# Relative-position softmax on one core: rows of one late chunk are dealt to the DMA engines by list

## The chip, the cores and the metric

The kernel runs on one core of a Trainium2 chip. The core has a vector engine (DVE), a scalar engine (ACT), a general engine (POOL), a synchronizing engine (SP) that here issues the transfers, and 16 DMA engines that move the bytes between the chip's memory (HBM) and the core's own memory (SBUF, 128 partitions). The metric is the device time of one execution in microseconds. TensorE does nothing in this kernel.

## The reference

Logits of shape 2 x 8 x 2112 x 2112 (float32, 285 MB) get a bias that depends on the distance of row and column alone, clipped to 16 on both sides, and then a softmax along the last axis:

```python
rel = pos[:, None] - pos[None, :]
rel_clipped = np.clip(rel, -max_rel, max_rel) + max_rel
bias = rel_bias[:, rel_clipped].copy()
logits = logits + bias[None, :, :, :]
logits = logits - logits.max(axis=-1, keepdims=True)
exp = np.exp(logits)
return (exp / exp.sum(axis=-1, keepdims=True)).astype(np.float32)
```

Each element is read once and written once: 571 MB in all.

## The kernel before

There are 2 x 8 x 2112 = 33,792 rows of 2112 numbers. Each of the 128 partitions takes 264 consecutive rows (`ROWS`), and works through them in 44 chunks of six rows (`N`, `R`). So a chunk is a tile of 128 partitions x 12,672 numbers, 6.3 MB, and one partition's share of it is one contiguous run of 50,688 bytes in HBM; this text calls that a full row of the transfer. Four buffers `X[0]` to `X[3]` hold four chunks (`NBUF`); chunk n lives in buffer n mod 4.

For each chunk DVE adds the bias to the six rows and finds each row's negated maximum (`add`, line 177, one instruction per row on line 181), ACT takes the exponential and the row's sum (`exps`, line 186), and DVE multiplies by the reciprocal sums in two halves of three rows (`scale`, line 195). The bias strip of four chunks is copied from PSUM to `F` once per four chunks (`strip`, line 173).

SP issues the loads and stores, all into one hardware queue per DMA engine, in this order. It first issues six one-row-per-partition loads for chunk 0 and the loads of chunks 1 to 3 (lines 98 to 103). Chunk 0 is stored in two parts: five of its six rows by one transfer (line 219), and the sixth by 17 small transfers (`FAN`, lines 41 to 48 and 221 to 232), which take k = 15, 14, 13, ... partitions, nine apart, so that DMA engine 0 gets 17 of these small rows and engine 15 none. The loop on line 233 then alternates: the store of the next chunk (which waits on `scaled` for six rows), a wait for the store before it to have landed (`st[b]`), and the load of the chunk that takes that buffer. POOL does the waiting for the parts of chunk 0's store (lines 114 to 117) and then adds 16 to `st[0]`, which lets SP issue the first reload. After the loop, lines 238 to 241 store chunks 41 and 42 whole and chunk 43 in two halves of three rows. Lines 242 to 244 wait until everything has landed.

So the transfers on the queue alternate store and load through the whole kernel, and at the end they are: store 40, load 43, store 41, store 42, and the two halves of 43. A transfer over 128 partitions gives each of the 16 DMA engines eight full rows.

## Time and profile before

| | |
|---|---|
| median of 3 runs | 1331.54 us (1331.24 to 1331.57) |
| the profiled execution | 1331.3 us |
| its span, first to last instruction | 1329.5 us |
| DVE busy | 976.7 us (73%) |
| ACT busy | 575.2 us (43%) |
| POOL busy | 0.4 us |
| moved by DMA | 571.12 MB, mean 430 GB/s |

Beside the table, the profile offers views that the prediction quotes. The page shows, in 40 slices of the span, the share of time in which the 16 DMA engines were busy (a 9 is 90% or more), and for each DMA queue its packets, MB and share. A row on a stretch gives its start and end, its length, the busy time of DVE, ACT and POOL with the number of instructions, the granted TensorE clock, the busy share of the DMA engines and the GB/s moved. A row of a timeline gives start, duration, engine, source line, operation, what is written and read, and, in brackets, idle time before it. "SPq" is SP's instruction stream: its issue of a transfer takes some tenths of a microsecond, while the transfer itself goes on in the queue. A row of the waits gives who waited for whom, the total, the number and the longest.

### The profile page before, as it was taken

To read this page: it belongs to the slowest core of one execution; us is meant where nothing else is said; L and a number is where in the kernel's file an instruction comes from. 1 tells how busy PE (TensorE), PEld (TensorE's weight loads), DVE (VectorE), ACT (ScalarE), POOL (GpSimd) and SP (SyncE) were. 2 spreads that over 40 slices of the span, in tenths; PEclk is the share of its full clock that TensorE was granted. 3 is DMA by queue.
4 is the path that set the end of the run, shared out by engine and by line. 5 is a ranking of instruction groups with operands and counts; after the bars stand their busy time and mean duration, and the time that the engine had idled before them with its cause. 6 is when DMAs were issued, how large, how long until landed. Compare 5 with 4: busy or idle time off the path is not lost. (4 is left out here: it accounts for less than half of the span.)

```text
span 1329.5 us, 2477 instructions
## 1 busy us (share of the span) xinstructions
DVE 976.7 (73%) x911; ACT 575.2 (43%) x539; POOL 0.4 (0%) x6
## 2 busy tenths in 40 slices
DVE  5998767777877776787778767677877776687772
ACT  2565333444444343345444333444444343345440
POOL 0000000000000000000000000000000000000000
DMA  9999999999999999999999999999999999999997
GB/s 391 427 426 424 436 430 433 438 433 435 432 435 435 433 436 430 436 433 435 430 433 439 433 433 427 439 435 432 433 432 438 430 433 430 436 430 436 438 432 337
DMA packets 13939, 571.12 MB, mean 430 GB/s; under 512 B 1648, under 2 KB 1776, under 8 KB 1776
## 3 DMA queue, kind: packets, MB, share of 16 engines
q1 hardware_dynamic: 13792, 570.96, 99.5%
q10 hardware_dynamic: 144, 0.14, 0.1%
q14 instruction: 3, 0.02, 0.0%
HBM read 285.61 MB, written 285.47 MB: 430 GB/s over the span
## 5 line engine op out<-in xcount | busy, mean ns | idle before, releaser
L181 DVE CUSTOM_DVE_ANT_0 X<-X,F 128x2112 f32<-128x2112 f32 x264 | 605.2, 2354 | 302.0 <-DVEq L85 302.0
L190 ACT ACTIVATE X<-X,nmax 128x2112 f32<-128x2112 f32 x264 | 541.7, 2052 | 538.2 <-ACTq L85 516.4
L202 DVE TENSOR_SCALAR X<-X,rec 128x2112 f32<-128x2112 f32 x264 | 332.5, 1316 | 13.2
L190 ACT ACT_TABLE_LOAD x11 | 14.1, 1283 | 185.8 <-ACTq L85 185.8
L190 ACT ACTIVATION_READ_ACCUMULATOR X<-X,nmax 128x1 f32 x264 | 49.2, 186 | 0.0
L175 DVE COPY F<-M 128x2135 f32 x11 | 26.1, 2375 | 6.6 <-DVEq L85 6.6
L181 DVE DVE_READ_ACCUMULATOR2_ANT nmax<- 128x1 f32 x264 | 21.7, 82 | 0.0
L198 DVE RECIPROCAL rec<-tot 128x3 f32<-128x3 f32 x88 | 15.0, 170 | 0.0
L146 DVE TENSOR_TENSOR F<-F 128x264 f32<-128x264 f32 x1 | 0.4, 435 | 4.9 <-DMA F<-in_rel_bias_dram 4.9
L167 DVE COPY M<-F 128x1848 f32<-128x1848 f32 x1 | 2.1, 2077 | 0.0
L133 DVE TENSOR_SCALAR ip<-ip 128x8 int32<-128x8 int32 x1 | 0.2, 172 | 1.3 <-POOL ip L113 1.3
L150 DVE TENSOR_REDUCE rbS<-F 128x33 f32<-128x264 f32 x1 | 0.6, 610 | 0.0
L164 DVE TENSOR_TENSOR M<-F 128x264 f32<-128x264 f32 x1 | 0.4, 441 | 0.0
L156 DVE TENSOR_TENSOR F<-F,rbS 128x264 f32<-128x264 f32 x1 | 0.4, 426 | 0.0
L143 DVE TENSOR_SCALAR F<-F 128x8 f32<-128x8 f32 x4 | 0.4, 167 | 0.0
L169 DVE COPY M<-rbS 128x247 f32<-128x247 f32 x1 | 0.4, 406 | 0.0
L154 DVE TENSOR_SCALAR F<-F,rbS 128x8 f32<-128x8 f32 x1 | 0.2, 231 | 0.0
L160 DVE SCALAR_TENSOR_TENSOR F<-F,rbS 128x8 f32<-128x8 f32 x1 | 0.2, 227 | 0.0
L155 DVE TENSOR_SCALAR F<-F,rbS 128x8 f32<-128x8 f32 x1 | 0.2, 225 | 0.0
L161 DVE SCALAR_TENSOR_TENSOR F<-F,rbS 128x8 f32<-128x8 f32 x1 | 0.2, 221 | 0.0
L136 DVE TENSOR_TENSOR F<-ip 128x8 f32<-128x8 int32 x1 | 0.2, 167 | 0.0
L139 DVE TENSOR_TENSOR F<-ip 128x8 f32<-128x8 int32 x1 | 0.2, 167 | 0.0
(9 smaller groups left out, 1.2 us busy)
## 6 DMA issues: line engine op xcount, KB each, us to landing
X<-in_logits_dram SPq DMA_DIRECT2D x43, 6336.0 KB, 44.7
out_dram<-X SPq DMA_DIRECT2D x42, 6336.0 KB, 52.8
X<-in_logits_dram SPq DMA_DIRECT2D x6, 1056.0 KB, 12.6
out_dram<-X SPq DMA_DIRECT2D x2, 3168.0 KB, 21.9
out_dram<-X SPq DMA_DIRECT2D x1, 5280.0 KB, 34.9
F<-in_rel_bias_dram ACTq DMA_DIRECT2D x1, 132.0 KB, 6.4
out_dram<-X SPq DMA_DIRECT2D x1, 123.8 KB
out_dram<-X SPq DMA_DIRECT2D x1, 115.5 KB
```

The costliest lines, as they stand in the source:

```text
L143: then(v.tensor_scalar(out=m, in0=dp, scalar1=0.0, scalar2=None, op0=op))
L146: then(v.tensor_tensor(out=view(F, 0, [[W, H], [1, W]]), in0=view(F, 0, [[W, H], [1, W]]), in1=view(F, SC + 3 * PB, [[1, H], [0, W]]), op= ...
L150: then(v.tensor_reduce(out=rbS[:, :], in_=view(F, 0, [[1, W], [W, H]]), axis=mybir.AxisListType.X, op=ALU.add))
L156: then(v.tensor_tensor(out=view(F, 0, [[W, PB], [1, W]]), in0=view(F, SC + 2 * PB, [[1, PB], [0, W]]), in1=view(rbS, W - 1, [[0, PB], [-1, ...
L164: then(v.tensor_tensor(out=view(M, U, [[ROWS, PB], [1, W]]), in0=view(F, 0, [[W, PB], [1, W]]), in1=view(F, SC + 8 * PB, [[1, PB], [0, W]] ...
L167: then(v.tensor_copy(out=view(M, U + W, [[ROWS, PB], [1, ROWS - W]]), in_=view(F, SC + 7 * PB, [[1, PB], [0, ROWS - W]])))
L169: then(v.tensor_copy(out=M[:, 0:U], in_=low.to_broadcast([P, U])))
L175: v.tensor_copy(out=F[:, :], in_=M[:, bass.ds(ROWS - STEP - j, FW)]).then_inc(dve, 1)
L181: v.tensor_tensor_reduce(out=x, in0=x, in1=F[:, STEP - 1 - r : STEP - 1 - r + S], scale=-1.0, scalar=BIG, op0=ALU.add, op1=ALU.min, accum_ ...
L190: nc.scalar.activation(out=x, in_=x, func=EXP, scale=-1.0, bias=nmax[:, r : r + 1], accum_out=tot[:, r : r + 1],).then_inc(expd, 1)
L198: v.reciprocal(out=rec[:, r0 : r0 + HALF], in_=tot[:, r0 : r0 + HALF]).then_inc(inv, 1)
L202: v.tensor_scalar_mul(out=x, in0=x, scalar1=rec[:, r : r + 1]).then_inc(scaled, 1)
```

## The change

The store of chunk 41, the last but two, is cut into parts. A partition p with p mod 8 in `OWN` = 0, 1, 2, 4, 5, 6 is stored by one of six SP transfers, each of 16 partitions that lie eight apart. The other 32 partitions (p mod 8 is 3 or 7) are stored by POOL with indirect transfers: each takes n partitions of the buffer, beginning at p0 and `lap` apart, and an index per partition that says which of the output's 5632 blocks of 12,672 numbers it goes to. An index past the last block (`FAR`) is skipped. `PLAN` lists five such transfers, each with the positions i whose index is kept: none of 112; 5 to 15 of 16 (partitions 43, 51, ...), twice, from 3 and from 7; eight of 16; and two of 16 (partitions 19 and 23). Together they keep 32 positions, each partition once.

POOL builds the five index columns in `sel` at the start, by an iota and two to five selects each, before it waits for chunk 0's store. Later it waits on `ready`, which SP raises when chunk 41 is scaled, at the place where SP issued the store before, and issues the five transfers. SP's wait for that store's landing counts six transfers now, and one more wait, on `soft`, covers the indirect ones. Nothing else is changed; DVE and ACT run the same instructions.

```diff
+    OWN = [0, 1, 2, 4, 5, 6]
+    PLAN = [
+        (112, 0, 1, []),
+        (16, 3, 8, range(5, 16)), (16, 7, 8, range(5, 16)),
+        (16, 3, 4, [0, 1, 2, 3, 6, 7, 8, 9]), (16, 9, 1, [10, 14]),
+    ]
+    FAR = 1 << 20
...
+        for w, (n, p0, lap, keep) in enumerate(PLAN):
+            col = sel[:, w : w + 1]
+            step(g.iota(col, pattern=[[0, 1]], base=p0 * N + N - 3, channel_multiplier=lap * N))
+            a, b = (min(keep), max(keep)) if keep else (P, P)
+            cuts = [(-a, 1, ALU.is_ge), (b, -1, ALU.is_ge)]
+            cuts += [(-i, 1, ALU.not_equal) for i in range(a, b) if i not in keep]
+            for base, mul, op in cuts:
+                g.wait_ge(pool, made[0])
+                step(g.affine_select(out=col, in_=col, pattern=[[0, 1]], base=base, channel_multiplier=mul,
+                                     compare_op=op, fill=float(FAR)))
+        take(g, pool, made[0])
         take(nc.gpsimd, main, 16)
         take(nc.gpsimd, fan[0], 16 * ((len(FAN) + 1) // 2))
         take(nc.gpsimd, fan[1], 16 * (len(FAN) // 2))
         nc.gpsimd.sem_inc(st[0], 16)
+        take(g, ready, 1)
+        blocks = out.rearrange("b h s t -> (b h s t)").rearrange("(n c) -> n c", c=R * S)
+        late = X[(N - 3) % NBUF]
+        LX = list(late.ap[0])[0]
+        for w, (n, p0, lap, keep) in enumerate(PLAN):
+            g.indirect_dma_start(
+                out=blocks, out_offset=bass.IndirectOffsetOnAxis(ap=sel[0:n, w : w + 1], axis=0),
+                in_=bass.AP(tensor=late.tensor, offset=late.offset + p0 * LX, ap=[[lap * LX, n], [1, R * S]]),
+                in_offset=None, bounds_check=P * N - 1, oob_is_err=False,
+            ).then_inc(soft, 16)
...
-        for n in range(N - NBUF + 1, N - 1):
-            store(n * R, n % NBUF)
+        take(nc.sync, scaled, R)
+        nc.sync.sem_inc(ready, 1)
+        for o in OWN:
+            nc.sync.dma_start(
+                out=bass.AP(
+                    tensor=out.tensor, offset=out.offset + (o * ROWS + (N - 3) * R) * S,
+                    ap=[[8 * ROWS * S, P // 8], [1, R * S]],
+                ),
+                in_=bass.AP(
+                    tensor=late.tensor, offset=late.offset + o * LX, ap=[[8 * LX, P // 8], [1, R * S]]
+                ),
+            ).then_inc(st[(N - 3) % NBUF], 16)
+        store((N - 2) * R, (N - 2) % NBUF)
         store((N - 1) * R, (N - 1) % NBUF, 0, HALF, landed)
         store((N - 1) * R, (N - 1) % NBUF, HALF, R - HALF, landed)
         for b in range(NBUF - 1):
-            take(nc.sync, st[(N + b) % NBUF], 16)
+            take(nc.sync, st[(N + b) % NBUF], 16 * len(OWN) if b == 1 else 16)
+    nc.sync.wait_ge(soft, nc.sync.to_reg(16 * len(PLAN)), synchronizes=[nc.sync.lower_ap(out)])
     nc.sync.wait_ge(landed, nc.sync.to_reg(32), synchronizes=[nc.sync.lower_ap(out)])
```

More of the change, by code (lines that the diff above doesn't have):

```diff
@@ L40 @@
     BIG = 3.0e38
+    OWN = [0, 1, 2, 4, 5, 6]
[5 more added lines that the diff above has]
+    FAR = 1 << 20
+    assert sorted(p0 + lap * i for n, p0, lap, keep in PLAN for i in keep) == [
+        p for p in range(P) if p % 8 not in OWN
+    ]
     LANES = 9
@@ L56 @@
     rec = io.tile([P, STEP], FP32, tag="rec", name="rec")
+    sel = io.tile([P, len(PLAN)], I32, tag="sel", name="sel")
     ip = io.tile([P, 3, PB], I32, tag="ip", name="ip")
@@ L79 @@
         dve = nc.alloc_semaphore("dve")
+        ready = nc.alloc_semaphore("ready")
+        pool = nc.alloc_semaphore("pool")
+        soft = tc.alloc_semaphore("soft")
         main = nc.alloc_semaphore("main")
@@ L113, with step @@
         nc.gpsimd.iota(ip[:, 2], pattern=[[1, PB]], base=0, channel_multiplier=0).then_inc(idx, 1)
+        g = nc.gpsimd
+        made = [0]
+        def step(ins):
+            made[0] += 1
+            ins.then_inc(pool, 1)
+        for w, (n, p0, lap, keep) in enumerate(PLAN):
[9 more added lines that the diff above has]
+        take(g, pool, made[0])
         take(nc.gpsimd, main, 16)
```

## The prediction

> **What bounds the kernel now.** I read three views: the page's DMA rows (is the queue ever empty?), the stretches at the end (how does it run dry?) and the timelines of SP and DVE (does compute hold a store back?). The page first:

> ```profile
> span 1329.5 us, 2477 instructions
> DMA  9999999999999999999999999999999999999997
> q1 hardware_dynamic: 13792, 570.96, 99.5%
> X<-in_logits_dram SPq DMA_DIRECT2D x43, 6336.0 KB, 44.7
> out_dram<-X SPq DMA_DIRECT2D x42, 6336.0 KB, 52.8
> ```

> All loads and stores are in queue q1, and it keeps 16 engines busy 99.5% of the span: bytes set the time, not DVE. Only the last slice is short of 9. The stretches (us, DVE busy, ACT busy, POOL busy, PEclk, DMA share, GB/s) show why:

> ```profile
> 130.00:500.00 370.00, 270.59 (x249) 157.14 (x149) 0.00 (x0) 1.00 1.00 434
> 1244.00:1305.00 61.00, 43.82 (x41) 25.78 (x24) 0.00 (x0) 1.00 1.00 432
> 1320.00:1321.00 1.00, 0.00 (x0) 0.00 (x0) 0.00 (x0) 1.00 0.77 329
> 1321.00:1322.00 1.00, 0.00 (x0) 0.00 (x0) 0.00 (x0) 1.00 0.59 253
> 1322.00:1323.00 1.00, 0.00 (x0) 0.00 (x0) 0.00 (x0) 1.00 0.41 177
> 1323.00:1324.00 1.00, 0.00 (x0) 0.00 (x0) 0.00 (x0) 1.00 0.41 177
> 1324.00:1325.00 1.00, 0.00 (x0) 0.00 (x0) 0.00 (x0) 1.00 0.24 101
> 1325.00:1326.00 1.00, 0.00 (x0) 0.00 (x0) 0.00 (x0) 1.00 0.18 76
> 1326.00:1327.00 1.00, 0.00 (x0) 0.00 (x0) 0.00 (x0) 1.00 0.06 25
> 1327.00:1328.50 1.50, 0.00 (x0) 0.00 (x0) 0.00 (x0) 1.00 0.04 17
> ```

> Times 16, the shares say that 12, 9, 7, 7, 4, 3 and 1 engines still work from 1320 on: the kernel ends with one engine alone. A full row (one partition's chunk, 50,688 bytes) costs an engine, at 434/16 = 27.1 GB/s, 1.87 us. The trace's packet records, which no view prints, say which engine is late. On one engine packets follow each other without a gap; every transfer gives each engine it uses its packets and then one of 4 bytes; and the 17 one-row transfers of chunk 0 give engine 0 seventeen packets, then 15, 14, 13, 12, 11, 10, 8, 7, 6, 5, 4, 3, 2, 1, 0, which names each chain. I followed the chains to the end:

> ```
> engine    0       1       2       3       4       5       6       7
> ends   1326.19 1325.95 1324.60 1325.72 1328.12 1324.18 1322.34 1321.89
> engine    8       9      10      11      12      13      14      15
> ends   1321.72 1320.89 1324.09 1320.88 1320.90 1320.87 1321.23 1321.99
> ```

> Their mean is 1323.2, so perfect balance would be worth 4.9 us. Engines 0 to 5 are late mostly by the one-row packets. Two have a cause of their own, seen in the time of their packets over the nominal one (1.872 us for a full row; sums in us, from the records):

> ```
> stretch       120-500   500-900   900-1300
> engine 4         1.15      1.80       1.46   (some 5 ns in every packet)
> engine 10        0.00      1.12       0.99   (ten single packets)
> engine 9         0.00      0.00       0.00
> ```

> **The change, part by part.**

> *Rows per engine.* The store of chunk 41 gives each engine eight rows. The six SP transfers give row i of 16 to engine i, six rows each. The lists name 32 more rows by position: engine 4 none, 0 to 3 one each, 5, 11, 12, 13, 15 two, 6 to 10 and 14 three (4 + 10 + 18 = 32). If position i is engine i there too, an engine's end moves by (count - 2) x 1.87:

> ```
> engine    0       1       2       3       4       5       6       7
> after  1324.32 1324.08 1322.73 1323.85 1324.38 1324.18 1324.21 1323.76
> engine    8       9      10      11      12      13      14      15
> after  1323.59 1322.76 1325.96 1320.88 1320.90 1320.87 1323.10 1321.99
> ```

> Engine 4 leaves the end, gaining 3.74; engine 10, late here and yet given a third row, is next. Last packet 1328.12 to 1325.96: -2.16 us. That one-row transfers go by position is in the records (engine 15 has none of the 17); that indirect ones do is not. [...]

> *Price of an indirect row.* None in this trace. Nearest: 1.87, the full row on q1. Below it nothing: a busy engine already moves at the rate of the 434 GB/s row. Above: the longest full-row packet of the records, 2.88. I take 1.87, since the 10,880 rows of that size in the records have a median of 1.87. At 2.88, engine 10 ends at 1324.09 - 3.74 + 3 x 2.88 = 1328.99, 0.9 later than now. Those ends, -2.2 and +0.9, go into the range.

> *The last load comes later.* SP and DVE at the end:

> ```profile
> 0.96 3.27 SPq L99 DMA_DIRECT2D X<-in_logits_dram  x6
> ...
> 1238.15 0.35 SPq L89 DMA_DIRECT2D X<-in_logits_dram  x1
> 1244.93 60.38 SPq L93 DMA_DIRECT2D out_dram<-X  x4
> 1271.08 3.78 DVE L202 TENSOR_SCALAR X<-X,rec 128x2112 f32<-128x2112 f32 x3
> 1283.08 2.36 DVE L181 CUSTOM_DVE_ANT_0 X<-X,F 128x2112 f32<-128x2112 f32 x1 [8.22 <-DVEq L85]
> 1300.77 0.17 DVE L198 RECIPROCAL rec<-tot 128x3 f32<-128x3 f32 x1
> 1301.09 3.78 DVE L202 TENSOR_SCALAR X<-X,rec 128x2112 f32<-128x2112 f32 x3
> ```

> Chunk 41 is scaled at 1244.9, while q1 still holds the store of 40 and the load of 43; the indirect rows go in between these, so each engine ends the load of 43 by count x 1.87 later. By the records engine 4 ends it last, at 1282.43, and engine 10 at 1279.18; after: engine 10 at 1284.8, the others by 1283.2. DVE starts chunk 43 some 2.3 later than 1283.08, and its first half, scaled and issued from 1301 on, goes out near 1303.3. A packet needs about 1.4 us from issue (first issue 0.96, first packet 2.35 in the records): 1304.7. The first engine needs it at 1305.86. Hidden, with 1.2 to spare; what it would cost without that cover is idle time on engines 11 to 13, which have 5 us in hand. The second half has over 5 us of cover.

> *SP and POOL.* Six issues take the place of one:

> ```profile
> 44.01 12.37 SPq L223 DMA_DIRECT2D out_dram<-X  x17
> 83.32 0.39 SPq L89 DMA_DIRECT2D X<-in_logits_dram  x1
> 1.13 0.14 POOL L113 IOTA ip<- 128x8 int32 x1
> SPq L244 <- DMA out_dram<-X: 14.6, 1, 14.6
> ```

> 12.37/17 = 0.73 each, 4.4 us, done by 1249.4. Behind them on SP is only the store of 42, whose data come at 1271.08 + 3.78 = 1274.9: nothing waits. POOL gets 5 iotas and 15 selects, 20 x 0.14 and a wait before each select, 3 to 6 us, ahead of its release of the first reload, which reached SP at 83.3: hidden by some 75 us of idle POOL, and all of those 6 us would show on the load of chunk 4 without it. The new wait of POOL for SP has only the five indirect issues behind it, whose rows any time up to 1300 would do; I bound five issues by SP's 0.35 to 0.73 each, 2 to 4 us, and let even 20 us pass. The first of them names no row, so it costs POOL time alone. SP's new wait for the indirect rows stands before the one for the last halves, which holds 14.6 us anyway: nothing. Nine or ten more completion packets of 9 ns per engine, and one more semaphore clear at the end: +0.15 together, an estimate from the records.

> *Sum.* -2.16 + 0.15 = -2.0 on the profiled execution's 1331.3, so 1329.3. That execution lies 0.24 under the median of 1331.54; against the median it is -2.2, or 0.17%. About 0.2% (2.7 us, 1328.9 and 1334.2) is what a measurement here can tell from no change.

> **Rivals.**

> *1. Engine 10 is not late.* Its 2 us came from ten stretched packets; the times of before can't tell if it is late in each run, as engine 4 hides it. Then the end is engine 4, 0 or 6 near 1324.4: -3.7 + 0.15, 1327.8. For it: the stretches fell on other engines in other spans. Against: five other engines carry a third row, and any may be hit instead.

> *2. Mixing stretches packets.* Indirect stores run beside a load, and q1's rows stretch as they did early on:

> ```profile
> 90.00:112.00 22.00, 20.61 (x19) 12.22 (x12) 0.00 (x0) 1.00 1.00 408
> ```

> (434 - 408)/434 x 22 = 1.3 us more per engine: 1330.6. Against: the queue here has long been in step, and other mixed stretches keep 432.

> *3. No rebalancing.* The rows do not go by position. If the refused indices drop out before rows are dealt, each list starts at engine 0: engines 0 and 1 get four rows, engine 4 three, and the last ends at 1328.12 + 1.87 = 1329.99, 1333.3. If each engine gets two, nothing changes: 1331.5. [...]

> *4. Slower: the rows eight apart run at half speed.* In the six SP transfers engines i and i + 4 read partitions 32 apart. If two engines reading such partitions halve each other, six rows cost 6 x 1.87 = 11.2 more: 1340.5. It decides from 0.8 more per row: then engine 10 ends 2.66 after 1328.12, at 2.67 per row. [...]

> **How the numbers follow.** Forecast, 1329.3 (1328.6 to 1330): 0.36. Rival 1: 0.34. Rival 2: 0.10. Rival 3: 0.09. Rival 4: 0.11. Range: rival 1 with 0.3 off, 1327.5, up to rival 3's 1333.3, which takes in the upper price of an indirect row (1331.3 + 0.9 + 0.15 = 1332.4); it leaves out rival 4 and some edges. The likeliest alone: 1328.6 to 1330.0. Faster by over 0.2%: nearly all of rival 1 and a quarter of the forecast, 0.41. Slower: rival 4 and a trace of others, 0.12. Within: 0.47.

> **What would show it.** A queue beside q1 with 32 rows of 50,688 bytes, 1.6 MB; shares after 1320 that stay high and then fall within 2 to 3 us; the last packet near 1326, engine 10's; DVE's first instruction of chunk 43 at 1284 to 1286; SP's issues of both last halves not behind an idle queue. Wrong would be: indirect rows well over 1.9 us, the six transfers slower than 11.2 us per engine, or a late engine that the list loads.

## The result: 0.57% slower

The changed kernel takes 1338.86 us (median of five, 1337.06 to 1342.12); the kernel before took 1331.26 beside it (1331.09 to 1331.57). The ratio is 1.0057, with a 95% interval of 1.0041 to 1.0074: slower, by 7.6 us. The profiled execution is one of the quicker ones, 1337.28 us, 5.98 more than the profiled execution of before. 1329.3 was forecast, and the range ended at 1333.3: the prediction was wrong, in sign too. What happened is in the main its rival 4, rows eight apart at half speed.

The page of the changed kernel, the lines that answer to those of before:

```profile
span 1335.5 us, 2534 instructions
DMA  9999999999999999999999999999999999999998
q1 hardware_dynamic: 13840, 569.33, 99.3%
q0 software_dynamic: 256, 1.62, 0.3%
HBM read 285.61 MB, written 292.77 MB: 433 GB/s over the span
```

The row of tenths says even less here than before: the engines are busy to the end, with an 8 where a 7 was. The 32 rows are on q0, 1.62 MB, as planned. The loss is seen only where busy time and bytes stand side by side, in the stretches of the changed kernel (columns as before: DMA share and GB/s are the last two):

```profile
1244.00:1305.00 61.00, 42.13 (x41) 25.78 (x24) 4.47 (x5) 1.00 1.00 380
1280.00:1290.00 10.00, 4.64 (x5) 2.15 (x2) 0.00 (x0) 1.00 1.02 340
1290.00:1300.00 10.00, 9.85 (x11) 9.34 (x9) 0.00 (x0) 1.00 1.05 289
1320.00:1321.00 1.00, 0.00 (x0) 0.00 (x0) 0.00 (x0) 1.00 0.94 406
1326.00:1327.00 1.00, 0.00 (x0) 0.00 (x0) 0.00 (x0) 1.00 0.94 406
1328.00:1329.00 1.00, 0.00 (x0) 0.00 (x0) 0.00 (x0) 1.00 0.65 279
1330.00:1331.00 1.00, 0.00 (x0) 0.00 (x0) 0.00 (x0) 1.00 0.47 203
1332.00:1333.00 1.00, 0.00 (x0) 0.00 (x0) 0.00 (x0) 1.00 0.12 51
```

From 1244 to 1305 the share is 1.00 as before, and the rate 380 GB/s instead of 432: (432 - 380)/432 x 61 = 7.3 us. The deepest hole, 289, lies where the six SP transfers of chunk 41 are. Before, the same two stretches of ten microseconds moved 421 and 446:

```profile
1280.00:1290.00 10.00, 6.92 (x7) 4.30 (x4) 0.00 (x0) 1.00 0.97 421
1290.00:1300.00 10.00, 9.85 (x11) 8.59 (x8) 0.00 (x0) 1.00 1.03 446
```

At the end the engines still run out one after another, over 9.3 us between the first and the last by the packet records (1324.20 to 1333.52; 7.3 before), only later. (A row counts each packet whole in the stretch in which it starts, so over 1 us the share gives the number of engines only roughly.)

The packet records name it. From 1240 us on, for full rows of 50,688 bytes on q1 (sum of the time over 1.872 us, rows over 2.2 us, longest row), and the end of the last data:

```
                      excess    slow rows   longest   last data
before                 0.6 us       0        2.15      1328.12
changed kernel       114.0 us      82        5.57      1333.52
```

114.0/16 = 7.1 us per engine, and the mean end of the 16 engines moved by about that, from 1323.22 to 1330.22. The median of the slow rows is 3.25 us; 31 of the 82 took 3.6 to 4.2, about twice 1.87. Not all of this lies in the six transfers: 12.1 of the 114.0 us, and 17 of the 82 slow rows (up to 3.16 us), belong to rows that began between 1268 and 1280, when no engine had reached the six transfers yet. They are rows of the load of chunk 43, and the kernel before has no slow ones there. The other 101 us came after 1280, 6.3 per engine. The last data come 5.4 later, and the ending after them takes 2.0 us instead of 1.4; together these make the 6.0.

What the prediction looked for in SP, POOL and DVE stands in the timelines of the changed kernel:

```profile
1245.47 5.29 SPq L283 DMA_DIRECT2D out_dram<-X  x6
1246.43 1.08 POOL L155 DMA_INDIRECT out_dram<-X,sel  x1 [1239.70 <-POOLq L99]
...
1251.27 0.85 POOL L155 DMA_INDIRECT out_dram<-X,sel  x1 [0.30 <-issue]
1285.36 2.36 DVE L223 CUSTOM_DVE_ANT_0 X<-X,F 128x2112 f32<-128x2112 f32 x1 [10.05 <-DVEq L99]
```

All of it is off the path: the issues are done by 1252.1, and chunk 43 starts at 1285.4, as foretold (1284 to 1286).

### The profile page after: what moved, and what is told of

It is laid out like the page before. It is cut to its first block, busy times and chain, and to the rows that moved or that the text cites. A ratio compares the mean times of both kernels' runs of the same rounds, so it can differ in the third digit from the quotient of the medians.

```text
span 1335.5 us, 2534 instructions
## 1 busy us (share of the span) xinstructions
DVE 976.7 (73%) x911; ACT 575.2 (43%) x539; POOL 8.2 (1%) x31
## 2 busy tenths in 40 slices
DMA packets 14245, 571.13 MB, mean 428 GB/s; under 512 B 1953, under 2 KB 2081, under 8 KB 2081
## 3 DMA queue, kind: packets, MB, share of 16 engines
q0 software_dynamic: 256, 1.62, 0.3%
HBM read 285.61 MB, written 292.77 MB: 433 GB/s over the span
## 5 line engine op out<-in xcount | busy, mean ns | idle before, releaser
L223 DVE CUSTOM_DVE_ANT_0 X<-X,F 128x2112 f32<-128x2112 f32 x264 | 605.2, 2354 | 304.9 <-DVEq L99 304.9
L244 DVE TENSOR_SCALAR X<-X,rec 128x2112 f32<-128x2112 f32 x264 | 332.5, 1316 | 13.2
L223 DVE DVE_READ_ACCUMULATOR2_ANT nmax<- 128x1 f32 x264 | 21.7, 82 | 0.0
L155 POOL DMA_INDIRECT out_dram<-X,sel x5 | 4.5, 893 | 1240.9 <-POOLq L99 1239.7
L143 POOL TENSOR_SCALAR_AFFINE_SELECT sel<-sel 128x1 int32<-128x1 int32 x15 | 2.9, 191 | 2.2 <-POOL sel L137 0.2
L198 DVE TENSOR_TENSOR F<-F,rbS 128x264 f32<-128x264 f32 x1 | 0.4, 426 | 0.0
L202 DVE SCALAR_TENSOR_TENSOR F<-F,rbS 128x8 f32<-128x8 f32 x1 | 0.2, 227 | 0.0
## 6 DMA issues: line engine op xcount, KB each, us to landing
X<-in_logits_dram SPq DMA_DIRECT2D x43, 6336.0 KB, 44.8
out_dram<-X SPq DMA_DIRECT2D x41, 6336.0 KB, 52.9
```

The costliest lines, as they stand in the source:

```text
L143: step(g.affine_select(out=col, in_=col, pattern=[[0, 1]], base=base, channel_multiplier=mul, compare_op=op, fill=float(FAR)))
L155: g.indirect_dma_start(out=blocks, out_offset=bass.IndirectOffsetOnAxis(ap=sel[0:n, w : w + 1], axis=0), in_=bass.AP(tensor=late.tensor, o ...
L223: v.tensor_tensor_reduce(out=x, in0=x, in1=F[:, STEP - 1 - r : STEP - 1 - r + S], scale=-1.0, scalar=BIG, op0=ALU.add, op1=ALU.min, accum_ ...
L244: v.tensor_scalar_mul(out=x, in0=x, scalar1=rec[:, r : r + 1]).then_inc(scaled, 1)
```

## The experiments

All kernels below ran once, but for f1 (four runs) and f2 (ten). The runs of before beside them lay between 1330.52 and 1332.0 us.

### Strided rows without the lists, and which side counts

Four kernels store chunk 41 by eight SP transfers, with no indirect ones. They differ in the distance of the partitions read (from SBUF) and of the places written (in HBM). e2 to e4 leave 16 of the 128 rows of chunk 41 out, and e2 and e3 write rows to other places than they belong. In outline (SRC and DST stand for 8 or 9, ROWS_ for the number of rows, 16 or 14; the waits are left out):

```diff
-        for n in range(N - NBUF + 1, N - 1):
-            store(n * R, n % NBUF)
+        for o in range(8):
+            nc.sync.dma_start(
+                out=bass.AP(..., ap=[[DST * ROWS * S, ROWS_], [1, R * S]]),
+                in_=bass.AP(..., ap=[[SRC * LX, ROWS_], [1, R * S]]),
+            ).then_inc(st[(N - 3) % NBUF], 16)
+        store((N - 2) * R, (N - 2) % NBUF)
```

> Before, with the store of chunk 41 cut into eight SP transfers of 16 partitions eight apart; no indirect transfers. Source theory (two DMA engines that read partitions 32 apart at the same time halve each other): full rows of this store take up to 3.7 us where both work at it, eight rows per engine instead of six, so some 7 to 9 us more than before, 1338 to 1340. Destination theory (16 engines that write 8 partitions' regions apart in HBM collide): the same here. One-row theory (a transfer with one row per engine is dear by itself): the same. Mixing theory (the indirect rows among the load disturb the queue, and the slow rows follow from that): no slow rows, 1331.3 to 1331.8.

> As the one before, but each of the eight transfers has 14 rows, read from partitions nine apart and written to the regions of partitions eight apart, so 16 regions of chunk 41 are not written, the others hold other partitions' rows, and engines 14 and 15 get none. Source theory: full rows stay at 1.87 us and the time at that of before, 1331.3 or up to 0.5 below. Destination theory: rows of 2.5 to 4 us, 1337 to 1340. One-row theory: the same as the destination theory.

> As the one before with the two strides changed about: 14 rows read from partitions eight apart, written to regions nine apart (16 regions not written, rows in other places). Source theory: rows of up to 3.7 us, 1337 to 1340. Destination theory: 1.87 us rows and 1331.3. One-row theory: slow.

> Both strides nine, 14 rows in each of eight transfers (16 regions not written). Source and destination theory: 1.87 us rows, 1331.3. One-row theory: slow, 1337 to 1340. If this is fast and the two before are both slow, both strides matter.

```
                          time     before   excess of full rows   slow rows
e1  16 rows, 8 and 8    1342.37   1332.0       195.5 us              104
e3  14 rows, 8 to 9     1341.73   1332.0       168.7                  89
e2  14 rows, 9 to 8     1340.15   1332.0        73.5                  39
e4  14 rows, 9 to 9     1340.43   1332.0        74.4                  40
```

The lists aren't needed for the loss: e1 has none and loses most. Whether the places written are eight or nine apart doesn't matter (e2 and e4 agree, 73.5 and 74.4 us, and so do e1 and e3 per row stored, 195.5/128 = 1.53 and 168.7/112 = 1.51); on the side read it does (e3 against e4, 168.7 and 74.4). That nine apart is slow as well was a surprise, since rows of one such transfer share no group of partitions in the sense below. Engines that are a few rows out of step can share one, across transfers; that this is the cause in e2 and e4 is argued, no run isolates it.

### Own groups against shared groups

Two kernels store 64 rows of chunk 41 in eight transfers of eight rows, and leave the upper 64 partitions of the chunk out. Four apart, engines 0 to 7 read 0 to 3, 4 to 7, and so on, and later the same partitions plus 32: each stays in a set of eight partitions {4g to 4g+3, 32+4g to 32+4g+3}, called a group here. Eight apart, engines i and i + 4 read the same group.

```diff
-        for n in range(N - NBUF + 1, N - 1):
-            store(n * R, n % NBUF)
+        for o in [0, 1, 2, 3, 32, 33, 34, 35]:    # e6: range(8)
+            ... ap=[[4 * LX, 8], [1, R * S]] ...  # e6: 8 * LX
```

> Before, with chunk 41 stored by eight SP transfers of eight partitions four apart (o + 4i, o = 0..3 and 32..35), so engine i of 0 to 7 reads only the partitions 4i..4i+3 and 32+4i..32+4i+3, which no other engine reads; partitions 64 to 127 of this chunk are not written and engines 8 to 15 get nothing. Shared-source theory (two engines that read the same group of eight partitions, {4i..4i+3, 32+4i..32+4i+3} or the same 64 higher, halve each other): every full row stays at 1.87 us, the late engines 0 to 7 end as before, 1331 to 1332. One-row theory (a transfer with one row per engine is slow wherever it reads): slow rows, 2.3 us and more, 1335 or later.

> The control to the one before: the same engines, counts and regions left out, but partitions eight apart (o + 8i, o = 0..7), so engines i and i + 4 read the same group of eight. Shared-source theory: rows of up to 3.74 us, eight per engine, 1338 to 1345. One-row theory: the same time as the one before. If both are fast, the slow rows need all 16 engines.

e5 took 1331.68 and e6 1343.61 us (before: 1331.3). From 1240 us on, e5 has no full row over 2.2 us, and e6 has 54. The stretch from 1290 to 1300, first of e5, then of e6:

```profile
1290.00:1300.00 10.00, 9.85 (x11) 9.47 (x10) 0.00 (x0) 1.00 0.54 233
```

```profile
1290.00:1300.00 10.00, 9.85 (x11) 9.49 (x9) 0.00 (x0) 1.00 0.50 132
```

In both about half of the engines work, with nearly the same work on DVE and ACT beside them. In e5 they move 233 GB/s, in e6 132. This settles that it is neither the number of rows in a transfer nor the number of transfers, but whom an engine shares a group with.

### The packets that misled

What spoke against rival 4 were four packets of chunk 0 (8,448 bytes, 319 ns each by the records of before): in them engine 3 read partitions 29 and 30 while engine 6 read 60 and 61, of one group. Are small rows spared? h1 and h2 are e6 and e5 with each row cut in six.

```diff
         for o in [...]:
+            for r in range(R):
-                ... ap=[[8 * LX, 8], [1, R * S]] ...
+                ... offset + o * LX + r * S, ap=[[8 * LX, 8], [1, S]] ...   # h2: 4 * LX
```

> The kernel of e6 (eight rows eight apart for each offset, engines i and i + 4 reading the same group of partitions; partitions 64 to 127 of chunk 41 are not stored), with each full row of 50,688 bytes cut into six of 8,448, 48 transfers in place of eight. It asks why chunk 0's one-row packets of 8,448 bytes took 319 ns although two engines shared a group. Theory A, sharing halves two engines whatever the size of the row: most packets at 0.6 us instead of 0.31, and 1341 to 1346 us as e6. Theory B, rows of 8,448 bytes are spared, because an engine does not keep its group long enough to meet the other: packets at 0.31 to 0.35 and 1331.5 to 1334 us. In between would say that the price hangs on how often the two engines happen to read at the same moment.

> The control for the run before it: the kernel of e5 (eight rows four apart, each of engines 0 to 7 in a group of its own; partitions 64 to 127 of chunk 41 are not stored), cut into 48 transfers in the same way. Both theories: packets of 8,448 bytes at 0.31 to 0.35 us; 48 completion packets of some 9 ns and 48 issues on SP add 0.5 us at most, so 1331.5 to 1333 us. If this one is as slow as the run before it, the cut itself costs the time and that run says nothing of sharing.

h1 took 1341.5, h2 1332.87 us (before: 1331.29). In h1 224 of 384 packets took over 400 ns, mostly 615 to 673; in h2 none did, and the longest was 349. So size doesn't spare them. Next, two engines that are in step, 0 and 1, got pairs of rows of a chosen distance:

```diff
+        for o in [0, 1, 2, 4, 5, 6, 8, 9]:        # i3: 0, 2, ..., 14
+            ... ap=[[32 * LX, 2], [1, R * S]] ...  # i2: 33, i3: 1, i4 and i5: 64
+        take(nc.sync, st[(N - 3) % NBUF], 16 * 8)  # i5 and i6 only
         store((N - 2) * R, (N - 2) % NBUF)
```

> Of chunk 41 only 16 rows are stored, by eight SP transfers of two rows each, so engines 0 and 1 move eight rows and the others none; the two rows of a transfer lie 32 partitions apart. Engines 0 and 1 end 0.24 us apart before, so they read the two rows of a transfer at the same time. Without any sharing the end is engine 0's, 1326.19 in place of 1328.12, so 1329.4 us. Both theories (the group of eight, or exactly 32 apart): rows at 3.6 to 4.2 us, and up to 1329.4 + 8 x 1.87 = 1344 us.

> The same with the two rows 33 partitions apart, in the same group of eight (0 and 33, 1 and 34, 2 and 35, 4 and 37, ...). The theory that the group of eight counts: rows at 3.6 to 4.2 us and up to 1344 us, as 32 apart. The theory that only partitions exactly 32 apart disturb each other, which would explain why chunk 0's packets were spared: rows at 1.87 and 1329.4 us.

> The same with the two rows next to each other (0 and 1, 2 and 3, ...), of the same four partitions. The theory of the group of eight: as slow as 32 apart, up to 1344 us. Exactly 32 apart: 1329.4 us.

> The same with the two rows 64 apart. The theory of the group of eight has the upper 64 partitions in groups of their own: 1329.4 us. If instead only the position within 32 counts, over all 128 partitions: rows at 3.6 to 4.2 us and up to 1344 us.

> The kernel of the pairs 64 apart (16 rows of chunk 41 stored, by engines 0 and 1), with SP waiting for these rows ahead of the store of chunk 42, so that no other engine stores beside them; the wait leaves the other engines idle. Groups of eight with the upper 64 partitions apart: all 16 rows at 1.87 us, from about 1281 to 1296, and about 1331 us. Position within 32 alone: rows at 3.6 to 4.2 us and some 15 us more, 1346.

> The same wait with the pairs 32 apart, the control. Both theories: rows at 3.6 to 4.2 us, none longer (the rows of 5 to 8 us of the run without the wait would have come from a third engine in the group), from about 1281 to 1311, and about 1346 us. If these rows are fast, it was store 42 beside them that slowed the pairs, and not the pair itself.

```
                            time     before   full rows over 2.2 us
i1  32 apart              1345.31   1331.87          14
i2  33 apart              1344.63   1331.87          14
i3  next to each other    1345.09   1331.87          15
i4  64 apart              1334.90   1331.87          12
i6  32 apart, alone       1343.08   1331.4           14 of the 16 pair rows
i5  64 apart, alone       1329.52   1331.4            0 of the 16 pair rows
```

Distance 32, 33 and 1 cost nearly the same (13.4, 12.8 and 13.2 us over before), so the group of eight counts, not one partition. (Here the places written move with the partitions read; that the side read counts rests on e1 to e4.) i4 fitted neither number: too slow for rows that share nothing, too fast for rows that do. Other engines were storing chunk 42 beside it, and some of these, it was supposed, read the same groups; i5 was then built to test it. With a wait that holds that store back, the pair is alone, and the answer is clean: 32 apart, every row but the first of each engine is slow (2.4 to 4.2 us), 64 apart none is (1.87). The stretch from 1284 to 1294, when only these two engines moved rows, of i5 and of i6:

```profile
1284.00:1294.00 10.00, 10.00 (x9) 7.37 (x7) 0.00 (x0) 1.00 0.12 51
```

```profile
1284.00:1294.00 10.00, 10.00 (x9) 7.31 (x7) 0.00 (x0) 1.00 0.14 30
```

Two engines, 0.12 to 0.14 of 16: 51 GB/s from two groups, 30 from one, little more than one engine's 27. This is the price of sharing in one row.

Why the four packets of chunk 0 were spared stays open. Two things were excluded, their size (h1) and their distance of 31 (as 1 and 33 are slow). i6 points at the length of the stretch: there the first rows of both engines began at 1280.65 and 1280.71, in one group, and both took 1.87 us; only the rows behind them were slow. In chunk 0 only two of the 128 packets were slow (586 and 531 ns), and the second is partition 31, the last that engine 3 read in the group that it shared with engine 6. So 1.8 us of sharing at the start passed unseen in i6, and chunk 0's packets shared for less, two of 0.32 us per engine. That this is why they were spared is argued, not shown.

### The empty list

e7 leaves out the first list, whose 112 indices are all refused.

```diff
     PLAN = [
-        (112, 0, 1, []),
```

> The changed kernel without the list of 112 refused indices. Its 4-byte packets, seven per engine, took turns with full rows of the main queue and so held the indirect rows back by some 13 us, until the load of chunk 43 ran. Without it the indirect rows come from about 1250 on, beside the store of chunk 40. Shared-source theory: they then read groups that other engines are storing from, and rows of both slow down: 5 to 20 us more in the sum over the 16 engines, the time up by 0 to 1.5 against the changed kernel's 1337.1 to 1342.1. Theory that only the six transfers matter: the same rows, only earlier, and the same time.

It took 1343.89 us in one run (before: 1331.3), more than any run of the changed kernel (1342.12). In the changed kernel q0 holds 256 packets: 32 full rows and 224 of 4 bytes, which are 144 refused indices (112 and 32) and 80 completions. So a refused index isn't dropped: it leaves a packet. By the records the queues take turns on an engine, about one 4-byte packet of q0 per full row of q1 (130 such packets and 117 full rows began between 1251 and 1264.7), and eight such turns hold the 32 rows back to 1264.8 to 1284.2, beside the load of chunk 43; 28 of the 32 took 1.87 to 2.2 us. Without the list they ran from 1250.4 to 1270.9, beside the store of chunk 40, and 15 of 32 were slow. So the list that names no row is a delay, and by this one run a useful one. It is not the store beside as such that does the harm: in f2 (below), 41 half rows of the lists ran between 1250 and 1262 beside the store of chunk 40 as well, each engine in its own group, and lost 0.2 us in all, where 26 rows of e7 lost 18.6 in the same stretch. Nor was the load of chunk 43 left alone in the changed kernel: 12.1 us of its rows' time went beside the lists or just behind them (see the result), against 0.4 in f2, both between 1268 and 1280. What stretched them was not tested.

### 96 partitions in one transfer

f1 drops the strided transfers: partitions 0 to 95 go in one SP transfer, 96 to 127 by lists with the same count per engine, but that engines 10 and 14 give their third row to 11 and 12.

```diff
-        (16, 3, 8, range(5, 16)), (16, 7, 8, range(5, 16)),
-        (16, 3, 4, [0, 1, 2, 3, 6, 7, 8, 9]), (16, 9, 1, [10, 14]),
+        (16, 96, 2, range(5, 16)), (16, 97, 2, range(5, 16)),
+        (16, 96, 1, [0, 1, 2, 3, 6, 7, 8, 9]), (16, 89, 1, [11, 12]),
...
-        for o in OWN:
-            nc.sync.dma_start(...)
+        nc.sync.dma_start(out=bass.AP(..., ap=[[ROWS * S, 96], [1, R * S]]), in_=late[0:96, :])
```

> The changed kernel with the six SP transfers replaced by one transfer of partitions 0 to 95 (six rows per engine), and the lists taking partitions 96 to 127 with the same number of rows per engine but for engines 10 and 14, which give their third row to 11 and 12. If a transfer of 96 partitions gives each engine partitions that no other engine reads, as the whole store does: no slow rows, last packet near 1324.5, 1327.5 to 1328.5, faster than before by 0.2 to 0.3%. If it deals runs of six neighbours, so that groups are shared: rows of 2 to 3.7 us, 1333 to 1338. If the indirect rows themselves are the cost: no better than the changed kernel.

1338.69 us (1337.39 to 1340.46) against 1331.3, ratio 1.0057 (1.0040 to 1.0074): no better. 36 rows of q1 and six of the lists were slow, 60.1 and 14.9 us. One transfer is no protection; the store of 128 partitions has no slow rows (none of before's from 1240 us on), f1 with one of 96 has 36. Which partitions each engine reads in either of them no run shows.

### The same idea in own groups

f2 keeps the balancing and takes the sharing away. The first half (three of the six rows) of chunk 41 is stored whole, over 128 partitions. Of the second half, partitions 0 to 31 go in four SP transfers of eight rows four apart, as in e5; 32 to 127 by lists whose position i is mostly a partition of engine i's own group, and which leave out engine 4.

```diff
-        (112, 0, 1, []),
-        (16, 3, 8, range(5, 16)), (16, 7, 8, range(5, 16)),
-        (16, 3, 4, [0, 1, 2, 3, 6, 7, 8, 9]), (16, 9, 1, [10, 14]),
+        (16, 32, 4, [0, 1, 2, 3, *range(5, 16)]), (16, 33, 4, [0, 1, 2, 3, *range(5, 16)]),
+        (16, 34, 4, [2, *range(5, 16)]), (16, 35, 4, range(5, 16)),
+        (16, 20, 2, [7, 9, 13, 15]), (16, 21, 2, [7, 9, 11, 13, 14]), (16, 36, 1, [12, 15]),
+        *((16, 64 + o, 4, range(8, 16)) for o in range(4)),
...
+        nc.sync.dma_start(out=rows(out, (N - 3) * R, HALF), in_=late[:, 0 : HALF * S])
-        for o in OWN:
+        for o in range(4):
-            ... ap=[[8 * LX, P // 8], [1, R * S]] ...
+            ... ap=[[4 * LX, 8], [1, HALF * S]] ...
```

> A version in which no two engines store from the same group of eight partitions at once: three of chunk 41's six rows go out by one transfer of 128 partitions; of the other three rows, partitions 0 to 31 go by four SP transfers of eight partitions four apart (engines 0 to 7, own groups), and partitions 32 to 127 by eleven lists of half runs (25,344 bytes, 0.94 us). Eight lists give each engine only partitions of its own group; three lists take four half runs from engine 4, two each from 0, 1, 3 and one from 2, and give them to 7, 9, 11 to 15, at a time when the owners load. Shared-source theory: no row over 2.2 us but perhaps a few of the moved ones; by the ends of before, engine 4 at 1324.4 and 0 at 1324.3 are last; with some 0.8 for more completions and a longer ending, 1327.8 to 1329.0, and not above 1330.5. If indirect rows beside the main queue have a cost of their own (packets stretched by the mixing), 1331 or more with slow rows that share no group.

1328.33 us (ten runs, 1327.81 to 1329.34) against 1331.38 (1330.52 to 1332.0): ratio 0.9979 (0.9969 to 0.9989), 3.05 us faster than before, and faster than both kernels. Its stretches:

```profile
1244.00:1305.00 61.00, 42.55 (x41) 25.78 (x24) 14.22 (x11) 1.00 1.00 432
1290.00:1300.00 10.00, 9.85 (x11) 9.48 (x10) 0.00 (x0) 1.00 1.04 449
1320.00:1321.00 1.00, 0.00 (x0) 0.00 (x0) 0.00 (x0) 1.00 0.94 406
1322.00:1323.00 1.00, 0.00 (x0) 0.00 (x0) 0.00 (x0) 1.00 0.53 228
1324.00:1325.00 1.00, 0.00 (x0) 0.00 (x0) 0.00 (x0) 1.00 0.00 0
```

The rate is back at 432, and the engines end within 2.7 us (1321.67 to 1324.41), where before it was 7.3. These are the shares "that stay high and then fall within 2 to 3 us" which the prediction asked of the change. f2 also stores shorter rows and has no empty list; neither spares a row by itself (h1, e7).

### No fan

Is the uneven end only the work of chunk 0's one-row packets? g1 stores chunk 0 of before in one transfer.

```diff
-        nc.sync.dma_start(out=rows(out, 0, R - 1), in_=X[0][:, 0 : (R - 1) * S]).then_inc(main, 16)
-        for i, (k, g, lane) in enumerate(FAN):
-            ...
+        nc.sync.dma_start(out=rows(out, 0, R), in_=X[0][:, :]).then_inc(main, 16)
```

> Before, with chunk 0 stored by one transfer instead of five rows and 17 small transfers, so the engines are not staggered on purpose. It tells where the spread of the ends comes from. If the small transfers make it (engine 0 gets 17, engine 15 none: 5.3 us), the ends lie closer, with engine 4 alone some 3.5 us late; the time then is the same or up to 3 us less, unless engines in step stretch each other's packets, which would cost some us over the whole span (1333 to 1345).

1330.3 us in one run against 1331.38. The stretch from 1324 to 1325 of it still shows engines at work:

```profile
1324.00:1325.00 1.00, 0.00 (x0) 0.00 (x0) 0.00 (x0) 1.00 0.24 101
```

By the packet records ten engines end between 1320.8 and 1321.6, six between 1324.8 and 1327.2, so part of the unevenness has another cause, which no run here names.

## Why the prediction was wrong

- *Rows per engine, the six SP rows at 1.87 us.* This is the step that failed. The table of ends gave every row, strided or not, the same 1.87; four packets of chunk 0 were taken as evidence that sharing costs nothing. 82 full rows took over 2.2 us, with a median of 3.25. After 1280 each engine lost 6.3 us; on six rows that is 1.05 each, so 2.9 us per row in place of 1.87 (some of it fell on the rows of chunk 42 behind them), and rival 4's point of decision, 2.67 per row, was passed. Its price was 11.2 us per engine, as if every row met another engine in its group; that doubling was an assumption that no run had shown, and many strided rows still took 1.87. The chance of 0.11 was too small: what stood against it was four packets of another size in a short stretch of sharing.
- *Rows per engine, the lists by position.* Right: f2, built on position i to engine i, ends at 1324.41 and spreads 2.7 us. That the lists' rows go by position no run had shown when -2.16 was worked out from it; so far as f2's end shows it, they do. Which engine is last, 10 or another (forecast against rival 1), wasn't decided.
- *Price of an indirect row.* Right: 28 of 32 rows within 1.87 to 2.2 us, the longest 2.57, under the upper end of 2.88; 2.6 us in all over 16 engines.
- *"The first of them names no row, so it costs POOL time alone."* Wrong: its refused indices take seven turns of the queue per engine, its completion one more, and hold the rows back some 13 us. That this cost time isn't shown; e7, without it, was slower.
- *The last load comes later.* Right: chunk 43 starts at 1285.36, and no engine pauses for the stores behind it. That the forecast was met so closely is partly luck, as rows of this load were stretched, which its working had at nothing.
- *SP and POOL.* Hidden, as said; the sizes were 5.29 us for six issues (4.4 forecast) and 5.7 for five indirect ones (2 to 4). The selects of the start were done by 6.7 us, long before chunk 0's store.
- *Ending.* +0.6 us in place of +0.15.
- *Rivals.* Rival 2 (mixing) occurred in part, or something like it: q1's rows of the load of 43, beside the lists and just behind them, lost 12.1 us, 0.8 per engine, where 1.3 was its price. In f2, which has lists too, the same rows lost 0.4 in all, so a list beside a load is not enough for it; the cause stays open. Rival 3, no rebalancing, isn't borne out at the end of this kernel: f2 stores chunk 41 in parts and wins 3.05 us, because it fills idle time of engines that end early.

So the mechanism of the gain was right and is worth what was said of it (-2.2 forecast; f2, which deals half rows, -3.05); the way in which the change cut the other 96 rows cost some three times that.

## What to carry to other kernels

## What the runs showed of the hardware beyond what was expected

- A refused index of an indirect transfer leaves a 4-byte packet on q0 (224 such packets: 144 refused indices and 80 completions), which takes a turn against a 50,688-byte row of q1 (130 of them beside 117 full rows between 1251 and 1264.7). The profile page's HBM count takes each refused index for a full row: 292.77 MB written instead of 285.47, and 144 x 50,688 bytes are 7.30 MB, while the DMA bytes stand at 571.13 MB.
- Beside the load of chunk 43, 28 of the 32 indirect rows of the changed kernel took 1.87 to 2.2 us; beside the store of chunk 40, 15 of e7's 32 were slow, up to 4.0 us. The load's own rows did lose time (17 over 2.2 us between 1268 and 1280, up to 3.16); f2 has one such row, of 2.29.
- In i6 two engines in one group were not slow at once: the first row of each took 1.87 us, and the rows behind it 2.4 to 4.2.
- In i5, with the wait ahead of the store of chunk 42, the last data came at 1326.43, though two engines alone stored 16 rows for 15 us; that the wait brought all 16 engines into step is the author's estimate of the cause. With 112 rows fewer to store it is no kernel to compare, and a wait of this kind was not tried with the whole work.
